# A four-layer hybrid decoder trunk on one core: recurrent mixer reordered, half of the attention's output weights left unsplit, convolution taps shared out anew

## The chip, the core and the metric

The kernel runs on one core of one Trainium2 chip. The metric is device time in microseconds (us) of one execution. The core has a matrix engine (PE, with its weight loads shown apart as PEld), a vector engine (DVE), an activation engine (ACT), a GpSimd engine (POOL) and a queue that issues transfers (SP). Each engine works through its own instructions in order; semaphores tie them together.

## What is computed

The input is x, 256 tokens by 1024 channels, batch 1. Each of four layers does

```
x = x + 0.5 * SwiGLU_1(RMSNorm(x))
x = x + Mixer(RMSNorm(x))
x = x + 0.5 * SwiGLU_2(RMSNorm(x))
```

The mixers are, in layer order, a recurrent block, forgetting attention, a causal convolution module, and a recurrent block again. SwiGLU has 2816 hidden channels. The recurrent mixer makes gate and u by one projection, runs a causal 4-tap convolution over u, computes two sigmoid gates per channel from 128x128 blocks, a decay a and a drive b, the scan h[t] = a[t] h[t-1] + b[t], and projects h * gelu(gate) out. The attention has 16 heads of 64 channels, an RMS norm on each head's q and k, and a bias from cumulated log forget gates. The convolution module gates one half of a projection by the sigmoid of the other, applies a causal depthwise convolution of 31 taps, a layer norm and a silu, and projects out.

## The kernel before, in words

**Layout.** Channels lie on the 128 partitions and tokens run along a row: x is four tiles of [128, 2, 256] (eight groups of 128 channels). Sublayer norms are folded in: products run on x times the norm's weight, and 1/rms is applied to the result.

**Weights and Feed (lines 62 to 151).** All weights come as one stream of 1 MB chunks of [128, 2048], in the order of use. A normal chunk is loaded to `wr` (3 buffers) and split in two pieces of 1024 columns: `high` (line 109, ACT) writes a rounded part `wh`, `low` (line 112, DVE) the rest `wl` (5 buffers each). Products with split operands are sums of hi*hi, hi*lo and lo*hi (lines 318, 320, 341, 373). A chunk in `whole` (lines 92 to 98) is loaded straight into a `wh` buffer and used unsplit by line 367, one matmul in place of three. `PLAIN = (0, 2)` says for which mixers (0 recurrent, 1 attention, 2 convolution) the first two of four output chunks are whole. `fill(lag)` prepares chunks until there are 5 - lag ahead of use, each piece high then low; `high(lag)` begins one chunk at most, issues both highs and returns a function that issues both lows; `steps` does one piece at a time. The load of chunk i+4 is issued after the last low of chunk i. SP carries all loads in that order.

**Start (lines 177 to 193).** x and the first chunk arrive in pieces. For each of four x tiles ACT makes the rounded x (line 233) and its square (236), DVE the rest (241) and the sum of squares (247). The sum is needed after the first 16 matmul pairs (norm_stat, line 284).

**SwiGLU (ffn, line 415)** is the bulk of the time: 22 input units and 11 output chunks, eight times.

**Recurrent mixer (rg, line 585).** Eight input units (`in_unit`, 48 matmuls each): units 0 to 3 give u, 4 to 7 the gate. Python order is the order on every engine. After unit j come `lift` (597, DVE), `first_tap` (602, ACT), `taps` (608, DVE), `gates` (615 PE, 616 and 618 ACT), `decay` (625, 626, 628, ACT), `recip` (633 to 638 DVE, 639 ACT); then two square roots (706) and the gelus (655) on ACT, `drive` (648 and the scans of 650, DVE). `finish` (731) multiplies gate and h (716, DVE), splits the last four products, and runs the output projection: units k = 0 to 3 use the whole chunks (367), 4 to 7 split ones (373), with `feed.fill(1)` after each k.

**Attention (fox, line 773).** Values first (822), then q and k pair by pair (units 0 to 5), evacuated by ACT (883 to 885). Head norms: `qk_stat` (890) multiplies the 512 squares by a selector of 32 columns, `qk_rows` (894, ACT) copies the rows out, `qk_turn` transposes them (899) and computes 1/rms on DVE. `heads` (1027) runs eight heads as a pipeline of scores, softmax (944 to 950), normalise (963), transposes (970), product with v (981, 983) and y (988 ACT, 989 DVE). The first eight heads have units 6 and 7 woven in on PE (`late_qk`), and weight pieces on ACT and DVE (`side`, one piece per step from step 3). The second eight have output units 2 to 4 woven in. A unit's result sits in one of three banks (`pr`), which the bias tiles of later heads use in turn.

**Convolution (conv, line 1079).** Eight input units. Channel tiles 4 to 7 are convolved on PE as 31 products with diagonal matrices (1127; ACT makes them, 1093), tiles 0 to 3 on DVE (1116, 1119). The loop at line 1182 issues rounds of six PE taps and five DVE taps. When tile 0 is done its mean over channels is taken (1188, PE), and from then on tiles are centred (1166), squared (1170) and summed on PE (1176). After the last sum come the variance and two table switches on ACT, then the output projection through `finish`.

Of the kernel before, what the change touches and what calls it, by code (L numbers as in the profile page):

```python
# [9 lines left out]
F32 = mybir.dt.float32  # L10
# [7 lines left out]
P = 128  # L18
# [21 lines left out]
PLAIN = (0, 2)  # L40
PE_TILES = (4, 5, 6, 7)
# [112 lines left out]
class Trunk:  # L154
# [3 lines left out]
    def build(self, pools):  # L158
# [23 lines left out]
        feed.load(RAW)  # L182
        nc.sync.dma_start(self.vec[:, KD:], self.ap["vec"][:, KD:])
# [37 lines left out]
    def prep_hi(self, b, s, js=(0, 1)):  # L221

        nc = self.nc
        if 0 in js:
            if b == 0:
# [4 lines left out]
            self.sq[b] = self.work.tile([P, 2, T], F32, tag="sq", bufs=2,  # L230
                                        name=f"sq{s}_{b}") if b else self.acc
        for j in js:
            nc.scalar.activation(self.xp[b][:, j, 0], self.x[b][:, j], AF.Copy,  # L233
                                 scale=self.v(f"norm{s}", 2 * b + j))
        j = slice(js[0], js[-1] + 1)
        nc.scalar.activation(self.sq[b][:, j], self.x[b][:, j], AF.Square)

    def prep_lo(self, b, s, js=(0, 1)):
        nc = self.nc
        for j in js:  # L240
# [3 lines left out]
                                           op0=ALU.mult, op1=ALU.subtract)  # L244
        if b:
# [339 lines left out]
    def rg(self, s, slot, last):  # L585
# [14 lines left out]
        def first_tap(j):  # L600
            for n in (2 * j, 2 * j + 1):
                nc.scalar.activation(uc[:, n], up[:, n, 0:T], AF.Identity,
                                     scale=self.v(f"rcw{slot}", n), bias=self.v(f"rcb{slot}", n))
# [26 lines left out]
        def recip(g):  # L630
# [8 lines left out]
            nc.scalar.activation(ee[:, n], ee[:, n], AF.Copy, scale=2.0, bias=-1.0)  # L639
# [27 lines left out]
        low = feed.high()  # L667
        lift(0)
        first_tap(0)
        low()  # L670
# [29 lines left out]
        evac_g(1)  # L700
        recip(2)
        decay(3)
        feed.fill(1)
# [27 lines left out]
    def finish(self, stages, s, bias=None, mid=None, whole=0):  # L731
# [29 lines left out]
        for k in range(KD - 2):  # L761
# [6 lines left out]
            self.feed.fill(1)  # L768
        c(KD - 1)
        self.feed.fill(1)  # L770
        self.out_tail([ys[KD - 2], ys[KD - 1]], s, bias)

    def fox(self, s, slot, last):
# [24 lines left out]
        hsel = carve(16, P).rearrange("p (i c) -> p i c", i=4)  # L798
        nc.gpsimd.memset(hsel, 0.0)
        for i in range(4):  # L800
            nc.gpsimd.memset(hsel[0:HD, i, 2 * i:2 * i + 1], 1.0)
            nc.gpsimd.memset(hsel[HD:P, i, 2 * i + 1:2 * i + 2], 1.0)
# [84 lines left out]
        def qk_stat(b):  # L887
            if b % 4 == 0:
                stp[b // 4] = self.st().rearrange("p (j t) -> p j t", j=2)
            nc.tensor.matmul(stp[b // 4][:FPAD], hsel[:, b % 4], sqs.pop(b),  # L890
                             start=(b % 4 == 0), stop=(b % 4 == 3))

        def qk_rows(g):
            nc.scalar.copy(rows[:FPAD], stp.pop(g)[:FPAD])

        def qk_turn(g, ps):
            ps = ps.rearrange("p j (t c) -> p (j t) c", t=TT)
            for i in range(2 * TT):
                nc.tensor.transpose(ps[:, i], rows[:, i // TT, (i % TT) * P:(i % TT + 1) * P],
                                    self.ident)  # L900
            z = self.tmp([P, 2, TT, 8], "qz")
            nc.vector.tensor_tensor(z, ps[:, :, :8].rearrange("p (j t) h -> p j t h", j=2),
                                    r2[:, None, :, None].to_broadcast([P, 2, TT, 8]), op=ALU.mult)
# [428 lines left out]
```

## Time and profile before

| | us |
|---|---|
| three runs: median (lowest to highest) | 1980.83 (1979.49 to 1981.73) |
| the profiled execution, its own time | 1979.21 |
| its span | 1977.5 |
| PE busy in the span | 1937.5 |
| DVE busy | 1440.4 |
| ACT busy | 1087.5 |

The span is what the engines' instructions cover; the profiled execution's own time is 1.7 us longer. Starts are counted from the start of the span. Matmuls are pipelined: a matmul's duration overlaps its neighbours, so the pace is read from one start to the next. An fp32 matmul that is not split shows as two instructions.

### The profile page before, as it was taken

Reading aid. Unit: us, or ns where it says so; the run is one execution under the profiler, and the core shown is the slowest. Engines: PE = TensorE matmul, PEld = TensorE weight load, DVE = VectorE, ACT = ScalarE, POOL = GpSimd, SP = SyncE. Lnnn points to the kernel's source line nnn. Section 1 sums busy time; section 2 is a strip of 40 time slices with the busy share of each in tenths; the row PEclk is TensorE's granted clock in tenths of the full one; section 3 lists DMA queues with packets and bytes.
Section 4 is the critical chain, followed back from the end, with each engine's and each line's share of the span. In section 5 each row is a group of like instructions: output and inputs, shape, how many; then the busy total and the mean of one; then the engine's idle time right before and its main releaser. Section 6 shows DMA issues by size and latency. Waiting matters only on the chain.

```text
span 1977.5 us, 28976 instructions
## 1 busy us (share of the span) xinstructions
PE 1937.5 (98%) x11450; PEld 1702.2 (86%) x11450; DVE 1440.4 (73%) x2538; ACT 1087.5 (55%) x1922; POOL 5.5 (0%) x25
## 2 busy tenths in 40 slices
PE   8999999999999998999999999989999999989999
PEld 7888988888888876888888889878888888988888
DVE  8985788767875667877587757858757876778773
ACT  6654666545654445656455546456545664566551
POOL 0000000000000000000000000000000000000000
PEclk9999999999999999999999999999999999999999
DMA  7655435545555323455555544015554554535551
GB/s 261 213 205 200 150 137 206 191 170 192 196 189 193 151 85 107 149 192 192 192 173 190 194 167 176 17 64 213 188 190 163 205 192 173 190 149 184 180 192 63
DMA packets 48665, 337.82 MB, mean 171 GB/s; under 512 B 5521, under 2 KB 6673, under 8 KB 8081
## 3 DMA queue, kind: packets, MB, share of 16 engines
q1 hardware_dynamic: 48528, 335.97, 47.2%
q8 instruction: 89, 1.46, 0.3%
q14 instruction: 48, 0.39, 0.1%
HBM read 334.90 MB, written 1.05 MB: 170 GB/s over the span
## 4 chain that ended last, share of the span: by engine, by line
PE 89%; DVE 6%; ACT 4%; issue 1%; DMA 0%; SPq 0%; ACTq 0%; DVEq 0%
PE b L318 49%; PE b L320 25%; PE b L341 4%; PE b L373 3%; PE b L1127 2%; DVE wl L112 2%; PE b L367 2%; PE b L822 1%; DVE s L1119 1%; ACT wh L109 1%; ACT s L1093 0%; ACT s L626 0%; PE b L890 0%; ACT s L625 0%; PE b L1176 0%
## 5 line engine op out<-in xcount | busy, mean ns | idle before, releaser
L318 PE MATMUL b<-xp,wh 128*128 128x512 f32 x2816 | 989.9, 396 | 7.2 <-ACT wh L109 7.2
L112 DVE TENSOR_TENSOR wl<-wr,wh 128x1024 fp32r<-128x1024 f32 (+1 forms) x622 | 743.8, 1216 | 191.6 <-ACT wh L109 191.3
L320 PE MATMUL b<-xp,wl 128*128 128x256 f32 x2816 | 790.5, 281 | 1.0 <-DVE wl L112 1.0
L109 ACT ACTIVATE wh<-wr 128x1024 fp32r<-128x1024 f32 (+1 forms) x622 | 635.7, 1047 | 165.5 <-PE b L318 83.8
L318 PEld LDWEIGHTS b<-xp,wh 128*128 128x128 f32 x2816 | 528.6, 188 | 130.5 <-ACT wh L109 7.5
L320 PEld LDWEIGHTS b<-xp,wl 128*128 128x128 f32 x2816 | 532.6, 189 | 2.6 <-DVE wl L112 2.6
L318 PE MATMUL b<-y,wh 128*128 128x512 f32 x1408 | 495.3, 395 | 0.0
L320 PE MATMUL b<-y,wl 128*128 128x256 f32 x1408 | 396.0, 281 | 0.0
L318 PEld LDWEIGHTS b<-y,wh 128*128 128x128 f32 x1408 | 264.5, 188 | 62.9
L441 ACT ACTIVATE bc<-b 128x256 f32<-128x256 f32 x352 | 117.4, 381 | 296.3 <-PE b L320 296.3
L320 PEld LDWEIGHTS b<-y,wl 128*128 128x128 f32 x1408 | 264.8, 188 | 0.0
L449 DVE TENSOR_TENSOR gu<-b,bc 128x256 f32<-128x256 f32 x352 | 132.8, 419 | 149.4 <-ACT bc L441 149.4
L341 PE MATMUL b<-xp,wh 128*128 128x256 f32 x1024 | 189.8, 287 | 5.1 <-ACT s L885 5.1
L341 PEld LDWEIGHTS b<-xp,wh 128*128 128x128 f32 x1024 | 160.1, 192 | 9.5 <-ACT s L885 6.0
L341 PE MATMUL b<-xp,wl 128*128 128x256 f32 x512 | 145.1, 283 | 0.0
L450 DVE TENSOR_TENSOR gu<-gu,ry 128x512 f32<-128x512 f32 x176 | 121.8, 692 | 6.0
L233 ACT ACTIVATE xp<-x,vec 128x256 fp32r<-128x256 f32 x96 | 46.7, 506 | 126.6 <-DVE x L494 105.3
L494 DVE SCALAR_TENSOR_TENSOR x<-b,x 128x256 f32<-128x256 f32 x128 | 53.2, 422 | 84.4 <-PE b L320 82.2
L453 ACT ACTIVATE sg<-gu 128x256 f32<-128x256 f32 x176 | 73.7, 419 | 51.2 <-DVE gu L450 41.7
L341 PEld LDWEIGHTS b<-xp,wl 128*128 128x128 f32 x512 | 98.1, 192 | 0.0
L433 DVE TENSOR_TENSOR y<-h,y 128x256 fp32r<-128x256 f32 x176 | 73.7, 419 | 3.9 <-ACT y L430 3.9
L462 DVE TENSOR_TENSOR h<-sg,gu 128x256 f32<-128x256 f32 x176 | 73.7, 418 | 1.0
(212 smaller groups left out, 1229.7 us busy)
## 6 DMA issues: line engine op xcount, KB each, us to landing
wr<-w SPq DMA_DIRECT2D x308, 1024.0 KB, 4.8
wh<-w SPq DMA_DIRECT2D x6, 1024.0 KB, 4.9
s<-wg SPq DMA_DIRECT2D x2, 1024.0 KB, 7.6
x<-xT SPq DMA_DIRECT2D x4, 256.0 KB, 5.9
wr<-w SPq DMA_DIRECT2D x4, 256.0 KB, 5.4
wr<-w SPq DMA_DIRECT2D x2, 512.0 KB, 7.5
out_dram<-x SPq DMA_DIRECT2D x8, 128.0 KB, 1.9
vec<-vec SPq DMA_DIRECT2D x1, 265.0 KB, 9.0
```

The source lines that it names most:

```text
L109: nc.scalar.activation(hi[:, c], raw[:, c], AF.Copy)
L112: nc.vector.tensor_tensor(lo[:, c], raw[:, c], hi[:, c].bitcast(F32), op=ALU.subtract)
L318: mm(bank, hi, y.rearrange("p a t -> p (a t)"), start=first, stop=False, skip_group_check=True)
L320: mm(bank[:, :T], lo, y[:, 0], start=False, stop=last, skip_group_check=True)
L341: nc.tensor.matmul(ps[:, j], w[:, k, j], m, start=(k == 0 and j == 0 and i == 0), stop=(k == KD - 1 and i == 2), skip_group_check=True)
L373: self.nc.tensor.matmul(self.o[m // 2][:, m % 2], wt[:, m * P:(m + 1) * P], mv, start=(first and m % 2 == 0 and i == 0), stop=(last and i ...
L433: nc.vector.tensor_tensor(ys[p][:, 1], hs.pop(p), ys[p][:, 0].bitcast(F32), op=ALU.subtract)
L441: nc.scalar.activation(bc[:, j], ps[j][:, T:], AF.Copy)
L449: nc.vector.tensor_tensor(gu[:, j], ps[j][:, :T], bc[:, j], op=ALU.add)
L450: nc.vector.tensor_tensor(gu, gu, self.r_b[:, None, :].to_broadcast([P, 2, T]), op=ALU.mult)
L453: nc.scalar.activation(sg, gu[:, 0], AF.Silu)
L462: nc.vector.tensor_tensor(h, sg, gu[:, 1], op=ALU.mult)
```

## The change

- `PLAIN` becomes (0, 1, 2): the first two output chunks of the attention are whole too. Its y of units 0 to 3 is one copy (ACT), without the DVE subtraction.
- Head norms: the squares become the stationary operand, 128 tokens at a time, and a selector of two columns the moving one. The sums come out token by token, DVE reads them straight from PSUM; `qk_rows` and the transposes go. `qk_turn(0)` moves from unit 5 to the end of unit 4, `qk_turn(1)` ahead of output unit 0.
- Convolution: PE takes tiles 5, 6, 7, 4 in this order, and of tile 4 the last 10 taps only; DVE takes the first 21, woven into tiles 2 and 3. DVE adds the two halves. A round has seven DVE taps, and a PE tile that ends in a round is centred a round later.
- Recurrent mixer: gates 0 and 1 follow unit 2 together, gates 2 follow unit 3, gates 3 unit 4. `first_tap` of j = 2, 3 and line 639 move from ACT to DVE. Weight chunks are begun at other points.
- `finish` prepares at most one chunk per k, both highs ahead of both lows; the attention's fills change alike.
- Start: a 1-element Copy on ACT first; squares and their sums after all four x tiles.

```diff
-PLAIN = (0, 2)
-PE_TILES = (4, 5, 6, 7)
+PLAIN = (0, 1, 2)
+PE_TILES = (5, 6, 7, 4)
+SHARED = 21
...
+        warm = self.tmp([P, 1], "warm")
+        nc.vector.memset(warm, 0.0)
+        nc.scalar.activation(warm, warm, AF.Copy)
...
         for b in range(4):
-            self.prep_hi(b, 0)
+            self.prep_hi(b, 0, squares=False)
             first[b][0]()
-            self.prep_lo(b, 0)
+            self.prep_lo(b, 0, squares=False)
             first[b][1]()
+        for b in range(4):
+            self.square(b, 0)
+            self.add_square(b)
...
+                if j < 2:
+                    nc.scalar.activation(uc[:, n], up[:, n, 0:T], AF.Identity, scale=w, bias=bias)
+                else:
+                    nc.vector.tensor_scalar(uc[:, n], up[:, n, 0:T], w, bias, op0=ALU.mult,
+                                            op1=ALU.add)
...
-            nc.scalar.activation(ee[:, n], ee[:, n], AF.Copy, scale=2.0, bias=-1.0)
+            nc.vector.tensor_scalar(ee[:, n], ee[:, n], 2.0, -1.0, op0=ALU.mult, op1=ALU.add)
...
         ps[1] = self.in_unit(wide)
-        low = feed.high()
         lift(0)
         first_tap(0)
-        low()
         lift(1)
         first_tap(1)
         taps(0)
         taps(1)
         ps[2] = self.in_unit()
-        pair_gates(0)
         low = feed.high()
         lift(2)
+        pair_gates(0)
+        pair_gates(1)
+        low()
         first_tap(2)
-        low()
         taps(2)
+        feed.high()()
         decay(0)
         ps[3] = self.in_unit()
-        pair_gates(1)
-        low = feed.high()
         lift(3)
+        pair_gates(2)
         first_tap(3)
+        taps(3)
         recip(0)
-        taps(3)
         decay(1)
         ps[4] = self.in_unit()
-        pair_gates(2)
-        low()
+        low = feed.high()
+        pair_gates(3)
         evac_g(0)
         recip(1)
+        low()
         decay(2)
-        feed.fill(1)
         ps[5] = self.in_unit()
-        pair_gates(3)
+        feed.high()
+        decay(3)
+        recip(2)
         evac_g(1)
-        recip(2)
-        decay(3)
-        feed.fill(1)
         recip(3)
...
             b(k + 2)
-            self.feed.fill(1)
+            self.feed.high()()
...
+            g, i = divmod(b, 4)
+            if i == 0:
+                stp[g] = self.st()[:, 32 * g:32 * g + 32].rearrange("p (j t h) -> p j t h", j=2,
+                                                                    t=TT)
+            sq = sqs.pop(b)
+            for j in range(2):
+                for tt in range(TT):
+                    nc.tensor.matmul(stp[g][:, j, tt, 2 * i:2 * i + 2],
+                                     sq[:, j, tt * P:(tt + 1) * P], hsel, start=True, stop=True)
...
+                if b < 4:
+                    ys[b] = self.tmp([P, T], "yp", 4)
+                    nc.scalar.activation(ys[b], ps, AF.Copy)
+                    return
...
         qk_stat(7)
-        qk_rows(1)
+        qk_turn(1)
         self.open_out()
-        first = self.out_steps(0, ys.pop(0))
-        pump(first, 4)
-        qk_turn(1, self.st().rearrange("p (j t) -> p j t", j=2))
-        pump(first, 9)
+        self.out_unit(0, ys.pop(0))
...
+        for k in range(SHARED):
+            dve_order.insert(2 * CK + 3 * k, (4, k))
...
+            if n == 4:
+                nc.vector.tensor_tensor(cv[:, n], cv[:, n], src, op=ALU.add)
+                src = cv[:, n]
...
-            new = run(ge, 6) + run(gd, 5)
+            new = run(ge, 6)
+            got = run(gd, 7)
             stats()
```

## Rows read from the trace of the kernel before

**Rows 1.** The page, part 1: busy time, share of the span, instructions, by engine.
```profile
PE 1937.5 (98%) x11450; PEld 1702.2 (86%) x11450; DVE 1440.4 (73%) x2538; ACT 1087.5 (55%) x1922; POOL 5.5 (0%) x25
```

**Rows 2.** Windows by stage: length, busy us of each engine, granted clock, DMA share, GB/s.
```profile
196.04:282.85 86.81, 81.92 (x583) 78.40 (x583) 68.01 (x118) 57.23 (x94) 0.00 (x0) 0.96 0.40 146
283.00:654.30 371.30, 371.30 (x2125) 324.56 (x2124) 273.03 (x438) 203.62 (x345) 0.00 (x0) 1.00 0.52 188
654.33:810.70 156.37, 148.42 (x960) 120.53 (x958) 104.38 (x293) 75.86 (x166) 4.13 (x15) 0.98 0.30 108
1182.34:1328.65 146.31, 136.90 (x834) 125.59 (x833) 101.59 (x224) 82.01 (x196) 0.00 (x0) 0.97 0.24 87
1700.23:1786.90 86.67, 80.94 (x583) 77.47 (x583) 68.00 (x118) 57.21 (x94) 0.00 (x0) 0.98 0.39 146
```

**Rows 3.** Timeline of PE around its waits [idle before, releaser].
```profile
254.54 17.00 PE L367 MATMUL b<-s,wh 128*128 128x256 f32 x64 [4.89 <-DVE s L716]
...
1758.74 15.77 PE L367 MATMUL b<-s,wh 128*128 128x256 f32 x64 [4.90 <-DVE s L716]
...
745.03 0.80 PE L341 MATMUL b<-xp,wh 128*128 128x256 f32 x2 [5.09 <-ACT s L885]
...
762.22 0.65 PE L981 MATMUL b<-s,s 128*64 128x256 f32 x2 [1.19 <-DVE yp L989]
...
1249.78 0.70 PE L1188 MATMUL b<-s,ones 128*128 128x256 f32 x2 [2.56 <-DVE s L1119]
1250.32 7.03 PE L1127 MATMUL b<-s,s 128*128 128x256 f32 x24
...
1294.20 0.70 PE L1176 MATMUL b<-s,ones 128*128 128x256 f32 x2 [0.58 <-DVE s L1166]
...
1301.62 15.71 PE L367 MATMUL b<-s,wh 128*128 128x256 f32 x64 [6.27 <-ACT s L1224]
```

**Rows 4.** The chain of waits: start, length, what.
```profile
271.54 11.31 PE b L373 x96
...
692.12 0.97 PE b L890 x2
...
1236.66 13.08 DVE s L1119 x33
...
1268.58 12.96 PE b L1127 x60
```

**Rows 5.** Timeline of DVE in the first recurrent mixer, 237 to 254 us.
```profile
237.75 0.69 DVE L645 TENSOR_TENSOR s<-b,ry 128x512 f32<-128x512 f32 x1 [2.15 <-PE b L615]
...
244.67 0.69 DVE L635 SCALAR_TENSOR_TENSOR s<-s,s 128x512 f32<-128x512 f32 x1 [2.87 <-ACT s L628]
...
249.88 1.22 DVE L648 TENSOR_TENSOR s<-s,s 128x1024 f32<-128x1024 f32 x1 [3.06 <-ACT s L706]
251.13 2.44 DVE L650 TENSOR_TENSOR_SCAN s<-s,s 128x256 f32<-128x256 f32 x4
```

**Rows 6.** Groups by line and shape, DVE: busy us, mean ns, idle before.
```profile
L112 DVE TENSOR_TENSOR wl<-wr,wh 128x1024 fp32r<-128x1024 f32 x618 | 741.1, 1220 | 191.0 <-ACT wh L109 190.7
...
L638 DVE TENSOR_TENSOR s<-s,s 128x512 f32<-128x512 f32 x8 | 5.5, 692 | 0.3
...
L1116 DVE TENSOR_SCALAR s<-s,vec 128x256 f32<-128x256 f32 x4 | 1.2, 351 | 0.0
```

**Rows 7.** Timeline of DVE in the attention's first eight heads.
```profile
740.68 1.23 DVE L112 TENSOR_TENSOR wl<-wr,wh 128x1024 fp32r<-128x1024 f32 x1 [0.22 <-ACT wh L109]
```

**Rows 8.** Timeline of PE around the token sums of a norm; weight loads by line.
```profile
201.64 0.50 PE L284 MATMUL b<-ones,acc 128*128 128x2 f32 x4
202.00 0.48 PE L341 MATMUL b<-xp,wh 128*128 128x256 f32 x2
...
L284 PEld LDWEIGHTS b<-ones,acc 128*128 128x128 f32 x48 | 6.5, 190 | 0.5
```

**Rows 9.** The chain of waits at the start of the span.
```profile
2.65 5.59 DMA x<-xT
```

More of the change, by code (lines that the diff above doesn't have):

```diff
@@ L219, in v, with prep_hi @@
         return self.vec[:, o + i:o + i + 1]
-    def prep_hi(self, b, s, js=(0, 1)):
+    def prep_hi(self, b, s, js=(0, 1), squares=True):
         nc = self.nc
@@ L234, in prep_hi, with square, prep_lo @@
                                  scale=self.v(f"norm{s}", 2 * b + j))
+        if squares:
+            self.square(b, s, js)
+    def square(self, b, s, js=(0, 1)):
+        if 0 in js:
+            self.sq[b] = self.work.tile([P, 2, T], F32, tag="sq", bufs=2,
+                                        name=f"sq{s}_{b}") if b else self.acc
         j = slice(js[0], js[-1] + 1)
-        nc.scalar.activation(self.sq[b][:, j], self.x[b][:, j], AF.Square)
-    def prep_lo(self, b, s, js=(0, 1)):
+        self.nc.scalar.activation(self.sq[b][:, j], self.x[b][:, j], AF.Square)
+    def prep_lo(self, b, s, js=(0, 1), squares=True):
         nc = self.nc
@@ L244, in prep_lo, with add_square @@
                                            op0=ALU.mult, op1=ALU.subtract)
+        if squares:
+            self.add_square(b, js)
+    def add_square(self, b, js=(0, 1)):
+        nc = self.nc
         if b:
@@ L767, in finish @@
             b(k + 2)
-            self.feed.fill(1)
+            self.feed.high()()
         c(KD - 1)
-        self.feed.fill(1)
+        self.feed.high()()
         self.out_tail([ys[KD - 2], ys[KD - 1]], s, bias)
@@ L797, in fox @@
                                     base=0, channel_multiplier=1)
-        hsel = carve(16, P).rearrange("p (i c) -> p i c", i=4)
+        hsel = carve(16, 2)
         nc.gpsimd.memset(hsel, 0.0)
-        for i in range(4):
-            nc.gpsimd.memset(hsel[0:HD, i, 2 * i:2 * i + 1], 1.0)
-            nc.gpsimd.memset(hsel[HD:P, i, 2 * i + 1:2 * i + 2], 1.0)
+        nc.gpsimd.memset(hsel[0:HD, 0:1], 1.0)
+        nc.gpsimd.memset(hsel[HD:P, 1:2], 1.0)
         rows = self.tmp([P, 2, T], "sq", 2)
@@ L887, in qk_stat, with qk_turn @@
         def qk_stat(b):
[L888 to L900, printed above, removed]
+            g, i = divmod(b, 4)
[7 more added lines that the diff above has]
+                                     sq[:, j, tt * P:(tt + 1) * P], hsel, start=True, stop=True)
+        def qk_turn(g):
             z = self.tmp([P, 2, TT, 8], "qz")
-            nc.vector.tensor_tensor(z, ps[:, :, :8].rearrange("p (j t) h -> p j t h", j=2),
-                                    r2[:, None, :, None].to_broadcast([P, 2, TT, 8]), op=ALU.mult)
+            nc.vector.tensor_tensor(z, stp.pop(g), r2[:, None, :, None].to_broadcast([P, 2, TT, 8]),
+                                    op=ALU.mult)
             nc.vector.tensor_scalar(z, z, 1.0 / HD, EPS, op0=ALU.mult, op1=ALU.add)
@@ L1007, in fox @@
         for b in range(6):
-            ps = self.in_unit({2: lambda: qk_turn(0, self.bank(2))} if b == 5 else None)
+            ps = self.in_unit()
             qk_evac(b, ps)
-            if b not in (4, 5):
-                feed.fill(1)
+            feed.high()()
             if b == 0:
@@ L1015, in fox @@
                 qk_stat(b - 1)
+            if b == 4:
+                qk_turn(0)
             if 1 <= b <= 4:
                 bias_pair(2 * b - 2, self.bank(b % 2))
-            if b == 4:
-                qk_rows(0)
         k_norm(0, [flat(f"o{i}", T) for i in range(4)])
@@ L1086, in conv @@
         room = [t[:, j * P:(j + 1) * P] for t in S[2:] for j in range(KD * PADC // P)]
-        pe_order = [(n, k) for n in PE_TILES for k in range(CK)]
+        pe_order = [(n, k) for n in PE_TILES for k in range(SHARED if n == 4 else 0, CK)]
         nd = [0]
@@ L1157, in conv @@
                 run(gd, 2)
-        done, pend, todo = 0, [], []
+        pend, todo = [], []
         cb = self.tmp([P, T], "cb")
@@ L1179, in stats @@
             pend.clear()
-        known = False
+        known, fresh, halves = False, [], 0
         while nst[0] < KD:
-            new = run(ge, 6) + run(gd, 5)
+            new = run(ge, 6)
+            got = run(gd, 7)
             stats()
-            todo += new
+            halves += got.count(4) + new.count(4)
+            for tiles in (got, new):
+                if 4 in tiles:
+                    tiles.remove(4)
+            if halves == 2:
+                new, halves = new + [4], 0
+            todo, fresh = todo + got + fresh, new
             if not known and 0 in todo:
```

16 lines of the change are left out of this document (7 added, 9 removed).

## The prediction, made before the changed kernel was run

> **What bounds the kernel now.** I read the page's busy shares first: PE is busy 1937.5 of 1977.5 us [rows 1], so only two things can shorten the run much, its 40 idle us and work that it needn't do or does slowly. The windows by stage come next. From one mixer to the next PE is busy 371.30 of 371.30 us at full clock [rows 2]: the SwiGLU stages are PE's own work, and the change leaves them alone. The four mixers hold 86.81, 156.37, 146.31 and 86.67 us, with granted clocks of 0.96 to 0.98 [rows 2]. The timeline of PE then shows where: 4.89 and 4.90 us ahead of the first output product of either recurrent mixer, 5.09 and 1.19 in the attention, 2.56 and 6.27 in the convolution [rows 3]. After a long wait the matmuls that follow run slowly. 64 instructions of line 367 took 17.00 us in the first recurrent mixer [rows 3]; the same kind of instruction (unsplit, 256 columns) in mid-convolution took 12.96 for 60, 0.216 each [rows 4], which makes 13.8 for 64. So the wait of 4.89 cost 3.2 us more at the lower of the clock's two levels (1.2 and 2.4 GHz), and in the second such mixer 15.77 - 13.8 = 1.9 more.
>
> **Recurrent mixers.** PE's work before the output projection ends at 254.54 - 4.89 = 249.65 us. The first product of line 716 is late because DVE had to wait 2.15, 2.87 and 3.06 us for gates, decay and square root [rows 5], 8.1 in sum: gates came late on PE, and ACT stood at line 639, waiting for DVE, before it could go on to the next decay. The new order issues all gates by the end of unit 4, and line 639 moves to DVE, so ACT never waits for DVE in mid-recip; I take these 8.1 us as gone. In exchange DVE gets four first taps at 0.35 (line 1116, same operation and size) and four scalings of 512 columns, which the trace doesn't show on DVE: between 0.35 (half the columns) and 0.69 (line 638, the same columns, two operands) [rows 6]. I take 0.5, nearer to the same operation; that is 1.4 + 2.0 = 3.4 us, bounds 2.8 to 4.2. DVE's end goes from 254.54 to about 249.9, PE waits some 0.3 us, and no slow stretch follows. Two pieces of a chunk (2 x 1.22 [rows 6]) also move from before unit 2 to after it; I take them as lying where DVE had waited for that unit, bounds 0 to 2.4. In the output projection the old order split three chunks after k = 0 in one go; now there is one per k, 2.4 us of DVE against 3.5 us of PE for an unsplit k (16 x 0.216) and 2.8 for a split one (11.31 / 4 [rows 4]), so the later products have their operands. On SP the two whole chunks go out one and two steps later, behind the load of the first split output chunk; their buffers were free after units 3 and 4, 10 us and more ahead of use. Work of PE in the mixer: 81.92 - 3.2 = 78.7; with the 0.3, 79.0. That saves 86.81 - 79.0 = **7.8** and 86.67 - 79.0 = **7.7** us. Bounds per mixer: 8.1 (no wait), or 2 (a wait of 3 us with its slow stretch).
>
> **Attention.** Unsplit weights cost PE time: 32 products at 2 x 0.216 = 0.43 in place of three at 11.31 / 96 = 0.118, 0.35 [rows 4]. That is +0.08 each, +2.6 in all, and on the path, since PE is full around them. What they spare is two chunks of splitting and four subtractions on ACT and DVE. The 5.09 us wait doesn't go with that: the woven steps still split a chunk at steps 3 and 4, now the next one, and there DVE itself waited for ACT's high (0.22 [rows 7]) before the scores behind which unit 6's evacuation stands. From step 7 on no pieces are left and y is one copy, so the 1.19 us, a wait for the subtraction [rows 3], goes: 1.2 (bounds 0 to 1.2). The head sums: one product took 0.97 us per pair [rows 4]; the nearest row to the new ones is line 284, the same operands, four instructions in 202.00 - 201.64 = 0.36 us [rows 8]. Eight of these are 0.72 per pair, -0.25 for seven pairs (the eighth falls into the wait): -1.75. Two times four transposes (line 899) go, taken at the same 0.09 each: -0.7. Sum: 2.6 - 1.2 - 1.75 - 0.7 = **-1.1**, bounds +0.2 to -8 (the 5.09 goes after all, with a slow stretch priced below at 1.85). The moved `qk_turn(0)` puts its small DVE steps ahead of one bias pair; PE's in-unit 5 covers them. The whole chunks leave ACT and DVE without work in units 4 and 5, and SP only waits there for buffers that units 3 and 4 free.
>
> For those sums a rule stands against the edit. The Trainium skill, "TensorE: Matmul & The Clock Gate", section "Step-by-step: what each phase is for", says that a weight load's time scales with the number of stationary columns, and these go from 32 to 128. The trace shows 190 ns for such a load [rows 8]; eight of them unhidden would be 1.5 us per pair, +4.4 in place of -1.75. Four such loads and their products fitted into 0.36 us, so they overlap, and the sum goes by that.
>
> **Convolution.** PE drops 21 of 124 taps, 21 x 0.43 = 9.1 us, but not all of it is on the path. Tile 0 is DVE's and is done at 1249.78 [rows 3] whatever PE does, as the taps ahead of it are the same. With five taps a round PE had issued 42 of its taps by then; with seven a round it has issued 30, and waits 12 x 0.43 = 5.2 us longer, 7.8. After that 73 taps are left in place of 82: 9 x 0.43 = 3.9 less. The old end also held a wait of 0.58 for the last tile's centring [rows 3]; now three other tiles' sums stand behind the last tap and hide the addition of tile 4's halves, its centring and its square: 4.5 less. DVE has then 83 taps at 13.08 / 33 = 0.40 [rows 4], eight centrings and the addition at no more than 0.5, 37 us. PE has 73 taps and eight times two sums of the same form, 89 x 0.43 = 38 us, and the slow stretch of 1.85 (24 instructions in 7.03 us, 5.18 at 0.216 each [rows 3, 4]), 40 us: DVE hides, by 3 us. The longer wait may lengthen that stretch by 0 to 1.3 (the one behind 4.89 us cost 3.2): I take 0.4. **-4.1**, bounds -4.5 to 0 (if DVE is the bound). The 6.27 us for variance and table loads stay.
>
> **Start.** Squares leave ACT's way and a table load comes earlier, but the second x tile lands only at 2.65 + 5.59 = 8.24 us [rows 9], and the first unit can't close before the same squares are summed, now behind everything else: 0, bounds -1 to +0.5.
>
> **Sum.** 7.8 + 7.7 + 1.1 + 4.1 = 20.7 us. The profiled execution took 1979.21, so it would take 1958.5; the median of the runs shown is 1.6 higher, which makes **1960**.
>
> **The rivals.** A is the forecast: 1956 to 1964, chance 0.60.
> B: the recurrent mixers' wait shrinks but stays. If the moved pieces count in full, DVE is 2.4 later and PE waits about 2.7 us. A wait of 2.56 was followed by a slow stretch [rows 3], so the clock's loss would stay: 2 x 2.2 in place of 15.5, about 1971. The DVE count is within 1 us of PE's end, which speaks for it; that nothing else is moved onto DVE speaks against. 0.16.
> C: the 5.09 us wait in the attention closes as well, 5.09 and 1.85 more: 1953. For it: DVE loses four subtractions, one of them right there; against: ACT's high ends no earlier. 0.08.
> D: the weight loads of the head sums (190 ns each) aren't hidden: 4.4 + 1.75 = 6.2 us above A, 1966. This trace's overlap speaks against it; 0.04. The same page's rule, taken alone, would have it so.
> E, on the other side: DVE becomes the bound. Its waits in the recurrent mixers stay 8.1 us because the order among them is set by ACT's decays and not by line 639; the added work of up to 4.2 us comes on top, and in the convolution DVE's 83 taps set the end. Then each recurrent mixer is 4.2 longer, the convolution gains nothing and the attention costs 0.2: 1980.8 + 8.6 = 1989.4. It decides if DVE's end falls after 254.5 us. For it: DVE is busy 68 of 86.8 us there [rows 2], no little; against: ACT is the one that was waited for. 0.06.
> F: the edits do as they say but the time only moves, the first mixers' waits turning up in the output projection (late chunks on the one-per-k plan) and in the attention: within 4 us of now. 0.06.
>
> **How the numbers follow.** About 0.2%, 4 us, is what a measurement of this kernel can tell from no change. Faster by more: A, B, C and D, 0.88; within: F, 0.06; slower: E, 0.06. The likeliest case gives 1960. The range takes in A, C, D and B: 1952 to 1972; E, F and the outer bounds are left out.
>
> **What would show it.** Right: no PE wait over 1 us ahead of line 367 in either recurrent mixer and 13.8 us for its 64 instructions; windows of about 79, 155, 142 and 79 us for the mixers; a PE wait near 7.8 us ahead of the convolution's mean; the 5 us wait in the attention still there. Wrong: line 716 (DVE) still releasing the first output product after 2 us or more; PE waiting for DVE at the end of the convolution's taps; eight head-sum instructions taking 1 us or more per pair.

## The result, and the profile after

The changed kernel takes 1946.49 us (median of 4 runs, 1945.12 to 1948.06), the kernel before in the same comparison 1981.18 us: a ratio of 0.9827, 95% interval 0.981 to 0.9844. That is 34.7 us faster. The forecast was 1960, with a range from 1952 to 1972: the sign is right, the size is 13.5 us short, and the range missed it by 5.5.

Page of the changed kernel, part 1, to be held against [rows 1]:

```profile
PE 1911.9 (98%) x11416; PEld 1698.4 (87%) x11416; DVE 1448.4 (75%) x2569; ACT 1069.4 (55%) x1880; POOL 3.8 (0%) x19
```

PE has 34 instructions less, yet it is 25.6 us less busy. The whole span, of one profiled execution each, lost 33.7 us (1977.5 to 1943.8), so only some 8 us came from idle time of PE. The windows by stage of the changed kernel show where (length, busy us of PE, PEld, DVE, ACT, POOL, granted clock, DMA share, GB/s); they answer to [rows 2]:

```profile
196.52:274.32 77.80, 77.80 (x583) 75.32 (x583) 70.65 (x127) 53.86 (x86) 0.00 (x0) 1.00 0.44 163
274.32:643.38 369.06, 369.06 (x2125) 325.64 (x2125) 273.16 (x439) 203.54 (x345) 0.00 (x0) 1.00 0.53 189
643.38:797.44 154.06, 148.06 (x968) 125.57 (x967) 98.68 (x286) 71.57 (x160) 2.44 (x9) 0.98 0.30 110
1166.48:1308.65 142.17, 128.11 (x791) 117.94 (x791) 110.05 (x246) 75.78 (x175) 0.00 (x0) 0.94 0.24 89
1677.72:1755.52 77.80, 77.80 (x584) 75.32 (x583) 70.61 (x127) 53.86 (x86) 0.00 (x0) 1.00 0.44 163
```

The mixers do about what was forecast: 77.80, 154.06, 142.17 and 77.80 us against "about 79, 155, 142 and 79". The second row is the surprise. The stage of two SwiGLU blocks between the first two mixers took 371.48 us before (282.85 to 654.33 in [rows 2]) and takes 369.06 now, with PE busy for all of it at full clock both times and not one instruction of it changed. Each of the three such stretches is 2.4 us shorter, and the last SwiGLU block, behind the last mixer, 2.3 (190.6 to 188.3): 9.6 us, most of the gap.

The timeline of PE in the changed kernel has these waits of a microsecond and more in the mixers [idle before, releaser], and the chain of waits (start, length, what) these stretches; they answer to [rows 3] and [rows 4]:

```profile
731.73 0.79 PE L358 MATMUL b<-xp,wh 128*128 128x256 f32 x2 [5.10 <-ACT s L903]
...
1233.70 1.22 PE L1217 MATMUL b<-s,ones 128*128 128x256 f32 x2 [8.74 <-DVE s L1137]
1280.32 16.82 PE L384 MATMUL b<-s,wh 128*128 128x256 f32 x64 [5.32 <-ACT s L1253]
```

```profile
248.99 13.81 PE b L384 x64
...
681.24 0.79 PE b L913 x8
...
752.13 7.01 PE b L384 x32
```

Line 384 is the old line 367. Ahead of it there is no wait left in either recurrent mixer and its 64 products take 13.81 us, as said. The wait of the attention stands (5.10, was 5.09); that of the convolution is 8.74 where 7.8 was forecast.

What the SwiGLU stages lost is pace. Groups by line of PE, first of the kernel before, then of the changed one (busy us, mean ns of one | idle before):

```profile
L318 PE MATMUL b<-xp,wh 128*128 128x512 f32 x2816 | 989.9, 396 | 7.2 <-ACT wh L109 7.2
...
L318 PE MATMUL b<-y,wh 128*128 128x512 f32 x1408 | 495.3, 395 | 0.0
```

```profile
L335 PE MATMUL b<-xp,wh 128*128 128x512 f32 x2816 | 981.3, 391 | 7.0 <-ACT wh L110 7.0
...
L335 PE MATMUL b<-y,wh 128*128 128x512 f32 x1408 | 494.7, 395 | 0.0
```

One such product is recorded until after the next pair has begun, so its busy time has no holes, and divided by the count it is the time of a pair (512 columns with the high weights, 256 with the low): 989.9 / 2816 = 351.5 ns before, 981.3 / 2816 = 348.5 now. Pairs that move y, in the same loop with the same weights, stay at 351.8 and 351.3. And the kernel before was not uniform. In the stretches 330 to 390 us (behind a mixer) and 500 to 560 us (ahead of one) its groups read

```profile
L318 PE MATMUL b<-xp,wh 128*128 128x512 f32 x171 | 60.5, 399 | 0.0
```

```profile
L318 PE MATMUL b<-xp,wh 128*128 128x512 f32 x174 | 60.4, 391 | 0.0
```

353.8 and 347.1 ns a pair: all SwiGLU blocks behind a mixer were slow, all ahead of one fast. In the changed kernel both stretches are at 347 ns:

```profile
L335 PE MATMUL b<-xp,wh 128*128 128x512 f32 x175 | 60.7, 390 | 0.0
```

```profile
L335 PE MATMUL b<-xp,wh 128*128 128x512 f32 x174 | 60.4, 390 | 0.0
```

DVE, ACT and the DMAs do the same in these stages in both kernels.

### The profile page after: what moved, and what is told of

Its sections match the earlier page's. It is cut to its first block, busy times and chain, and to the rows that moved or that the text cites. A ratio compares the mean times of both kernels' runs of the same rounds, so it can differ in the third digit from the quotient of the medians.

```text
span 1943.8 us, 28888 instructions
## 1 busy us (share of the span) xinstructions
PE 1911.9 (98%) x11416; PEld 1698.4 (87%) x11416; DVE 1448.4 (75%) x2569; ACT 1069.4 (55%) x1880; POOL 3.8 (0%) x19
## 3 DMA queue, kind: packets, MB, share of 16 engines
HBM read 334.90 MB, written 1.05 MB: 173 GB/s over the span
## 4 chain that ended last, share of the span: by engine, by line
PE 94%; DVE 3%; ACT 2%; DMA 0%; issue 0%; SPq 0%; DVEq 0%; ACTq 0%
PE b L335 49%; PE b L337 26%; PE b L358 7%; PE b L384 3%; PE b L390 2%; PE b L1146 2%; PE b L840 1%; DVE s L1137 1%; DVE wl L113 1%; PE b L636 1%; ACT wh L110 1%; ACT s L1109 0%; PE b L1198 0%; PE b L997 0%; DMA x<-xT 0%; PE b L321 0%
## 5 line engine op out<-in xcount | busy, mean ns | idle before, releaser
L335 PE MATMUL b<-xp,wh 128*128 128x512 f32 x2816 | 981.3, 391 | 7.0 <-ACT wh L110 7.0
L358 PE MATMUL b<-xp,wh 128*128 128x256 f32 x1024 | 184.7, 283 | 5.1 <-ACT s L903 5.1
```

The source lines that it names most:

```text
L335: mm(bank, hi, y.rearrange("p a t -> p (a t)"), start=first, stop=False, skip_group_check=True)
L358: nc.tensor.matmul(ps[:, j], w[:, k, j], m, start=(k == 0 and j == 0 and i == 0), stop=(k == KD - 1 and i == 2), skip_group_check=True)
```

## Experiments: is it where xp lies?

The change reserves its [128, 1] tile `warm` ahead of acc and xp. Tiles are laid out in steps of 32 bytes, so in every partition xp0 moves from byte 122432 to 122464; the weights (wh from 38464) and the six slabs with y (y0 at 170368) stay. Theory P: this place sets the pace. Rival Q: the instructions do, or what runs beside them.

```diff
 (kernel before)
         feed.load(RAW)
+        self.tmp([P, 1], "warm")
```

> The kernel before with one edit: a tile of [128, 1] under the name `warm` is reserved as the first tile of the work pool, with no instruction on it; it moves acc, sq and xp by 32 bytes in each partition (xp0 from 122432, a multiple of 64, to 122464). Theory P (place): products that move xp run faster in the changed kernel because its `warm` tile shifts xp by 32 bytes. Then line 318 and 320 on xp go from 351.6 ns a pair to about 348.5 (2816 pairs, -8.7 us), line 341 loses about 5.5 us over its 1536 instructions, and the time is about 1967 (1965 to 1969), with every wait of before still there. Rival Q (work): the pace comes from what the other engines do or from the order of the instructions; then nothing changes, 1981 (1979 to 1983) and 351.6 ns a pair.

The padded kernel before (e1): 1972.29 us, ratio 0.995 (0.9936 to 0.9965). Two windows of it, the first recurrent mixer and the stage behind:

```profile
195.76:282.24 86.48, 80.79 (x584) 77.14 (x583) 68.04 (x118) 57.30 (x94) 0.00 (x0) 0.96 0.39 147
282.24:651.28 369.04, 369.04 (x2126) 325.81 (x2125) 273.09 (x438) 203.49 (x345) 0.00 (x0) 1.00 0.53 189
```

No instruction was added, and the SwiGLU stages are those of the changed kernel. P holds for them, Q falls. But 9.0 us came, not 14: the recurrent mixer lost 0.3 us only. Its products on xp are faster too, but there DVE's late line was still waited for (5.62 us ahead of the output products, 4.89 before), and the gain turned into waiting. The attention and the convolution got no shorter either: 158.78 and 147.80 us in this execution, 156.53 and 146.31 before, with granted clocks of 0.97 and 0.95 against 0.98 and 0.97.

```diff
 (changed kernel)
-        warm = self.tmp([P, 1], "warm")
+        warm = self.slab.tile([P, KD * PADC], F32, tag="s0", bufs=1, name="warm0")[:, :1]
```

> The changed kernel with its early `warm` column taken from the slab of y0 in place of a tile of its own, so that acc, xp0 and xp1 lie where the kernel before has them (xp0 at 122432) and xp2, xp3 4096 bytes, a whole tile, below; every instruction of the change stays. Theory P (place): the SwiGLU stages behind a mixer go back to 353 ns a pair on xp (371.5 us from mixer to mixer in place of 369.05), line 358 to 120.0 ns each in place of 116.8, all of it on the path now that PE no longer waits in the recurrent mixers: rg stages 79.0, and the time is 1960 (1957 to 1962), which is what the forecast gave from the change's own steps. Rival Q (work): the change's instructions, not the place, make the pace; then 1946.5 (1945 to 1948). Rival R: the FFN's 9.7 us go back, the in-units' don't: 1956.

The changed kernel with xp0 and xp1 in their old place (e5; xp2 and xp3 lie a tile lower, at the same distance modulo 128): 1960.70 us (1958.00 to 1962.05), ratio 0.9896 (0.988 to 0.9912): P, and near the forecast's own number. All instructions of the change are in it. Windows of the first recurrent mixer, the stage behind it, the attention and the convolution:

```profile
198.91:277.65 78.74, 78.74 (x584) 76.25 (x583) 70.54 (x126) 53.76 (x86) 0.00 (x0) 1.00 0.44 161
277.65:649.13 371.48, 371.48 (x2126) 324.69 (x2125) 273.19 (x438) 203.77 (x346) 0.00 (x0) 1.00 0.52 188
649.13:805.63 156.50, 150.52 (x968) 128.10 (x967) 98.65 (x285) 71.51 (x160) 2.45 (x9) 0.96 0.29 108
...
1177.11:1319.30 142.19, 129.13 (x792) 118.96 (x791) 110.03 (x245) 75.71 (x175) 0.00 (x0) 0.95 0.24 89
```

So the place made 9.0 us of difference to the kernel before and 14.2 to the changed one. Not all of the 14.2 is the pace. Of the 16.5 us between the two profiled executions 9.6 lie in the SwiGLU blocks behind mixers, 1.9 in the recurrent mixers and some 2.5 ahead of the first mixer, where e5's first block ran slow though that of the kernel before ran fast. The last 2.4 lie in the attention, at a granted clock of 0.96 where the changed kernel had 0.98; that isn't the place, as a slow place (e2 below) has 153.76 us there. Next, which place, and against what? A control moves everything behind xp and sq by the same 32 bytes, xp not:

```diff
 (kernel before, behind the loop that makes the first xp)
             first[b][1]()
+        self.tmp([P, 1], "warm")
```

> The kernel before with the [128, 1] tile reserved behind xp and sq: nz, bc, gu, sg, h and the mixers' y pairs move by 32 bytes, acc, sq, xp, the weights and the slabs don't. P, it is xp's place against the weights that counts: 1981 (1979 to 1983), SwiGLU stages 371.5 from mixer to mixer. Rival S, it is the place of what ACT and DVE read and write beside PE: as with the pad ahead of xp, 1972.

The control (e7): 1980.07 us, ratio 0.9994 (0.9985 to 1.0004): no difference. What ACT and DVE work on in the SwiGLU stages is not it.

In the changed kernel a second tile ahead of `warm` moves xp by another 32 bytes and the slabs with it; one in the constants' pool moves the weights too:

```diff
 (changed kernel, first run)
+        self.tmp([P, 1], "pad")
         warm = self.tmp([P, 1], "warm")
 (changed kernel, second run)
+        c.tile([P, 1], F32, name="pad")
         warm = self.tmp([P, 1], "warm")
```

> The changed kernel with a second [128, 1] tile reserved ahead of `warm`: xp moves by another 32 bytes, back onto a multiple of 64 (122496), and the slabs behind the work pool (the SwiGLU's y pairs) move by 32 too, off a multiple of 64 (170400). P: products on xp go back to 351.6 ns a pair, +14 us; if the place counts for y as it does for xp, the 1408 pairs that move y gain 3.1 ns each, -4.4: 1956 (1954 to 1958), or 1960 if y is indifferent. Q: 1946.5 (1945 to 1948).

> The changed kernel with a [128, 1] tile reserved in the constants' pool, ahead of everything but x and vec: identity, weights, xp and slabs all move by 32 bytes, so that xp lies on a multiple of 64 again (122496), weights and y off it. P1, a product's pace is set by the place of the moved operand alone: pairs on xp 351.6, pairs on y 348: +14 - 4.4, 1956 (1954 to 1958). P2, it is set by the distance between weights and moved operand: all distances are as in the changed kernel, 1946.5 (1945 to 1948), pairs on xp 348.5. Q: 1946.5 as well, so P2 and Q are told apart by the other three runs.

The first (e2) took 1962.82 us (ratio 0.9902, 0.9887 to 0.9917), the second (e4) 1946.39 us (0.9819, 0.9802 to 0.9835). In both xp and y lie on the same bytes; only the weights differ. Groups by line of e2, then of e4:

```profile
L336 PE MATMUL b<-xp,wh 128*128 128x512 f32 x2816 | 1000.5, 397 | 6.5 <-ACT wh L110 6.5
...
L336 PE MATMUL b<-y,wh 128*128 128x512 f32 x1408 | 491.9, 393 | 0.0
```

```profile
L336 PE MATMUL b<-xp,wh 128*128 128x512 f32 x2816 | 981.8, 391 | 7.1 <-ACT wh L110 7.1
...
L336 PE MATMUL b<-y,wh 128*128 128x512 f32 x1408 | 494.7, 395 | 0.0
```

355.3 and 348.7 ns on xp, 349.4 and 351.3 on y. It is the distance between weights and moved operand (P2), not the operand's own place (P1): e4 moves both and has the changed kernel's paces again. My number for the first run, 1956, was too low, since I had taken a shift of 64 bytes for none.

How the distance counts was tried with more shifts: of xp and the slabs on the kernel before, of the slabs alone on the changed one.

```diff
 (kernel before; 64, 96 and 160 bytes ahead of xp)
+        self.tmp([P, 1], "pad"); self.tmp([P, 1], "warm")
+        self.tmp([P, 1], "pad"); self.tmp([P, 1], "pad2"); self.tmp([P, 1], "warm")
+        self.tmp([P, 25], "pad"); self.tmp([P, 1], "warm")
 (changed kernel; slabs by 32 and by 64 bytes)
+        self.slab.tile([P, 1], F32, tag="pad", bufs=1, name="pad")
+        self.slab.tile([P, 16], F32, tag="pad", bufs=1, name="pad")
```

> The kernel before with two [128, 1] tiles reserved at the head of the work pool, no instruction on them: xp0 at 122496, a multiple of 64 as in the kernel before (122432) and as in the run with the second pad; the slabs move by 32 bytes, as there. If being a multiple of 64 decides, xp pairs are slow again: 1981 less 4 for y, 1977 (1975 to 1982), SwiGLU stages at 353 ns a pair either behind each mixer only (as in the kernel before) or everywhere (as in the run with the second pad, then 1984). Rival: any shift breaks up what the kernel before happens to have; then as with one pad, 1972 less up to 3, 1969 to 1973.

> The kernel before with three [128, 1] tiles reserved at the head of the work pool, no instruction on them: xp0 at 122528, off a multiple of 64 as with one pad (122464), the slabs moved by 64 (170432). If half a line of 64 bytes between weights and moved operand is all that counts, xp is fast and y slow as with one pad: 1972 (1970 to 1974), 347 ns a pair in every SwiGLU stage, 369.05 us from mixer to mixer. Rival: finer or coarser places count; then another pace than 347, 353 or the mixture of the kernel before.

> The kernel before with 160 bytes reserved at the head of the work pool and no instruction on them: xp0 at 122592, which lies to 128 bytes as 122464 does (one pad, 347 ns a pair everywhere); the slabs move by 128. If places count modulo 128, this is the run with one pad again: 369.05 us from mixer to mixer, 347 ns a pair on xp, 351.1 on y, 1972 (1970 to 1974). Rival, a longer period: another pace, as with three pads, and a time of 1976 to 1986.

> The changed kernel with a [128, 1] tile reserved as the first of the slab pool: only the slabs move, by 32 bytes (y pairs from 170368, a multiple of 64, to 170400); xp and the weights stay where the changed kernel has them. P: pairs on xp keep 348.5 ns, pairs on y go from 351 to about 348, -4.4 us, and other products that move slabs gain a little: 1941.5 (1940 to 1943). Q: 1946.5 (1945 to 1948).

> The changed kernel with the slabs moved by 64 bytes in place of 32 (y pairs from 170432, a multiple of 64 as in the changed kernel), xp and weights unmoved. If the place modulo 64 is what counts for y, pairs on y take 351.1 ns again as in the changed kernel, and the time is 1946.5 (1945 to 1948). Rival, any move of the slabs helps: 349.3 ns and 1943.5.

The times, in us, and ratios: 64 bytes (e6) 1985.59, 1.0022 (1.0012 to 1.0032); 96 bytes (e10) 1981.35, 1.0003 (0.9993 to 1.0012); 160 bytes (e14) 1970.76, 0.9945 (0.9928 to 0.9961); slabs by 32 (e3) 1943.51, 0.9809 (0.9794 to 0.9823); slabs by 64 (e12) 1946.47, 0.9825 (0.981 to 0.984). The runs sort by the distance from weights to operand modulo 128 bytes (the weight tiles lie alike in this count; pace of a pair as busy / count over the whole run; for y the distance is that of the first slab, y0; "before" and "after" are the kernels before and after the change):

```
distance   pairs on xp, ns                                  pairs on y, ns, by the place of y0
  0        351.5 (before), 351.7 (e7), 352.5 (e5)           351.5 (e10), 351.5 (e12)
 32        348.5 (e1, after, e12), 348.2 (e14),             none
           348.7 (e4), 348.8 (e3)
 64        354.6 (e6), 355.3 (e2)                           351.3 (e1, after, e4), 351.6 (e14)
                                                            351.8 (before, e5, e7)
 96        352.1 (e10)                                      349.5 (e3), 349.4 (e2, e6)
```

The y column mixes two distances. A slab takes 8 x 286 x 4 = 9152 bytes (line 419 of the kernel before), which is 64 more than a multiple of 128, so y1, y3 and y5 lie 64 bytes off from y0, y2 and y4 in this count. Taken apart, by the mean time from the start of one pair on y to the next (without the last 16 pairs of a block, which are taken in another order), the slabs read

```
run (place of y0, of y1)      y0, y2, y4, ns            y1, y3, y5, ns
after (64, 0)                 352.4, 352.5, 348.8       349.9, 351.1, 352.5
e12   (0, 64)                 350.8, 353.1, 350.9       351.0, 352.2, 348.7
e3    (96, 32)                352.2, 352.7, 350.3       346.5, 346.8, 346.4
before (64, 0)                353.1, 352.4, 348.8       351.5, 351.1, 352.5
e14   (64, 0)                 352.9, 348.9, 351.9       351.1, 353.1, 350.5
```

At 32 y is fast, as xp is (347.6 in the same measure); the slabs' shift by 32 gained it on three slabs of six, so the run fell short of the 348 ns and the 1941.5 us that were expected. A shift by 64 only exchanges the two groups' distances, so e12 couldn't tell 64 from 0. e4 has the changed kernel's paces slab by slab, within 0.1 ns. Elsewhere the distance modulo 128 doesn't settle the pace: e14 has every slab 128 bytes further than the kernel before, and y2 went from 352.4 to 348.9.

My "modulo 64" is refuted by xp at 32 and 96 (the run with 96 bytes was to be at 1972); with 64 bytes every SwiGLU block was slow, and the time 1.6 us above the 1984 that I had for this case. And the 160 bytes, predicted from the period of 128 before they ran, came out like 32 for xp: the window of that run between the first two mixers reads

```profile
282.95:652.11 369.16, 369.16 (x2126) 324.19 (x2125) 273.17 (x438) 203.76 (x346) 0.00 (x0) 1.00 0.53 189
```

Distance 0 alone has two paces, 347 and 353, by the stage (the two rows of the kernel before, 330 to 390 and 500 to 560 us); in e5, at the same distance, the first block was slow too. What puts a stage into one or the other was not tried, nor why a distance matters at all. The best layout found moves the slabs by 32 bytes: the stages between mixers are at 368.4 us and the time at 1943.51. Its interval overlaps that of the changed kernel, so the 3 us in the total are not shown; the pace of y is. Slabs of a size that is a multiple of 128, all at 32, would be worth some 4 us by an estimate from e3's row (12 of 22 y, 768 pairs, 5.1 ns each); that was not run.

## Experiments: the change's own parts

**Scaling back on ACT.** One edit of the recurrent mixer undone:

```diff
 (changed kernel, recip)
-            nc.vector.tensor_scalar(ee[:, n], ee[:, n], 2.0, -1.0, op0=ALU.mult, op1=ALU.add)
+            nc.scalar.activation(ee[:, n], ee[:, n], AF.Copy, scale=2.0, bias=-1.0)
```

> The changed kernel with one of the recurrent mixer's edits undone: the scaling by 2 and -1 at the end of each recip goes back from DVE to ACT. If that move is what lets ACT run ahead (my step: ACT stood there, waiting for DVE, before it could go on to the next decay), part of DVE's 8.1 us of waiting comes back: PE waits 2 us or more ahead of line 384, its 64 instructions take 15 us or more, the recurrent stages take 81 to 87 us in place of 77.8 and the time is 1953 to 1965. Rival: the order of gates and decays did it alone; PE is the bound, the stages stay at 77.8 and the time at 1946.5 (1945 to 1948).

1959.38 us, ratio 0.9893 (0.9878 to 0.9909), 12.9 above the changed kernel. Timelines of PE and of DVE in the first recurrent mixer:

```profile
252.74 16.83 PE L384 MATMUL b<-s,wh 128*128 128x256 f32 x64 [3.90 <-DVE s L735]
```

```profile
232.98 0.69 DVE L656 SCALAR_TENSOR_TENSOR s<-s,s 128x512 f32<-128x512 f32 x1 [1.33 <-ACT s L649]
...
239.61 0.69 DVE L656 SCALAR_TENSOR_TENSOR s<-s,s 128x512 f32<-128x512 f32 x1 [1.61 <-ACT s L649]
...
248.07 1.23 DVE L669 TENSOR_TENSOR s<-s,s 128x1024 f32<-128x1024 f32 x1 [3.06 <-ACT s L725]
```

And ACT, at the scalings of the first and the last group:

```profile
229.54 0.63 ACT L660 ACTIVATE s<-s 128x512 f32<-128x512 f32 x1 [3.76 <-DVE s L659]
...
245.04 0.63 ACT L660 ACTIVATE s<-s 128x512 f32<-128x512 f32 x1 [2.17 <-DVE s L659]
```

ACT stands behind DVE, DVE waits for ACT's decays and roots again ([rows 5] had 2.87 and 3.06 there), PE waits 3.90, the products behind take 3.0 us more than 13.81, and the stage takes 84.71 us. In the changed kernel none of these waits is there. So the new order of the gates needs this edit: without it the change is worth some 2 us a mixer (86.81 to 84.71, the place included), not 9. Whether the scaling's move would do without the new order was not run.

**The attention's unsplit weights**, taken out of the change, and put alone into the kernel before:

```diff
 (changed kernel: out; kernel before: the reverse)
-PLAIN = (0, 1, 2)
+PLAIN = (0, 2)
...
-                if b < 4:
-                    ys[b] = self.tmp([P, T], "yp", 4)
-                    nc.scalar.activation(ys[b], ps, AF.Copy)
-                    return
```

> The changed kernel with one of the attention's edits undone: the two chunks of its out projection are split again, and the first four y are pairs (three products of 0.118 us in place of two of 0.216). My terms for this edit: +2.6 for the slower form, -1.2 for a wait that went; undone, the attention goes from 154.05 to 152.7 us and the time to 1945.1 (1943.5 to 1946.5). Rival: the splitting that it spares ACT and DVE is worth more than the product time, and waits come back: the attention takes 156 us or more, the time is 1948 to 1952.

> The kernel before with one of the attention's edits alone: weights of the first half of its out projection unsplit and the first four y copied whole, everything else (the planned loads and splits, the head sums, the rest of the change) as before. My term: +2.6 for 32 products in the slower form, -1.2 for a wait that goes, so the attention from 156.5 to 157.9 us and the time from 1981 to 1982.4 (1981 to 1984). Rival, from the run with the split put back (which cost 7.6 us): the spared splitting is worth more than the products cost in any order of the work, and the attention falls to 150 to 154 us, the time to 1974 to 1979. Third: it is worth that only under the changed kernel's plan of whole chunks; then my term holds here and the two edits belong together.

Out: 1954.90 us, ratio 0.9865 (0.9849 to 0.9882), slower by 8.4 where 1.4 faster was expected, and 2.9 above the range of the rival that had it slower. Alone in the kernel before: 1981.70 us, ratio 1.0002 (0.9993 to 1.0011), no difference. Window of the attention, a wait of PE and what DVE did ahead of it, in the run with the split put back:

```profile
645.30:806.98 161.68, 150.73 (x1000) 129.23 (x999) 104.93 (x293) 75.43 (x164) 2.45 (x9) 0.95 0.30 105
```

```profile
715.87 1.97 PE L937 MATMUL b<-ident,s 128*128 128x128 f32 x8 [4.24 <-DVE s L931]
```

```profile
706.37 2.36 DVE L113 TENSOR_TENSOR wl<-wr,wh 128x1024 fp32r<-128x1024 f32 x2 [3.21 <-ACT wh L110]
708.65 0.18 DVE L918 TENSOR_TENSOR qz<-b,r 128x32 f32<-128x32 f32 x1
...
713.25 2.36 DVE L113 TENSOR_TENSOR wl<-wr,wh 128x1024 fp32r<-128x1024 f32 x2 [0.42 <-ACT wh L110]
715.53 0.89 DVE L931 COPY s<-rqk 128x256 f32<-128x256 f32 x4
```

The third theory of that pair fits: the change plans one whole chunk per unit, and without unsplit chunks those of units 4 and 5 put 2.36 us of splitting each on DVE, one ahead of the head norms' first step (line 918), one right ahead of the norm's scales (line 931) that the first heads wait for; in the changed kernel DVE splits nothing there. PE is idle 10.95 us in this attention, 6.00 in that of the changed kernel; the rest of the 7.6 us is slower products, at a granted clock of 0.95. The unsplit weights don't pay by themselves; the plan needs them. That the two splits make all of the loss is argued from this trace, not tried.

**More taps on DVE**, on top of the slabs' better place:

```diff
 (changed kernel with the slabs moved by 32 bytes)
-SHARED = 21
+SHARED = 25
```

> A candidate: the changed kernel with the slabs moved by 32 bytes (as in the run with the slab pad, 1943.5) and four more taps of tile 4 on DVE (SHARED 25 in place of 21). DVE waits 2.3 us for PE's last tap in the changed kernel; four taps are 1.7 us of PE and 1.6 of DVE, so the two end about together. Theory (PE's end sets the convolution's, as my forecast had it): the convolution's stage goes from 142.2 to 140.5 or 141.2 us, the time to 1942 (1940.5 to 1944). Rival (DVE is the bound from here): the stage takes 142.2 to 144, the time is 1943.5 to 1946.

1944.34 us, ratio 0.9812 (0.9797 to 0.9827). The convolution's window:

```profile
1168.04:1309.47 141.43, 126.81 (x784) 116.28 (x783) 111.60 (x249) 74.35 (x171) 0.00 (x0) 0.94 0.25 90
```

That is 1.05 us less than the same layout with 21 (142.48), as the theory wanted, but with 21 the stage took anything from 141.07 (e12) to 142.48 by layout. Inconclusive, and no better in total.

## Why the forecast fell short

**The step that failed** is in the first paragraph of the prediction: "the SwiGLU stages are PE's own work, and the change leaves them alone". The instructions were left alone; their operands were not. I priced the early `warm` by its table load and not by the 32 bytes that its tile takes, and no rival had it that untouched work runs at another pace. The term that I put at nothing measured 9.6 us in the SwiGLU blocks behind mixers and 1.9 in the recurrent mixers; with the 1.4 by which the attention's term was too small this is 12.9 of the missing 13.5. With xp put back the change takes 1960.70 us, 0.7 from the forecast. That nearness is in part luck: in e5's execution the first block lost 3.0 us against the kernel before and the attention, at the lower granted clock, gained nothing. A pace of 353.8 and one of 347.1 ns for the same products stood in the trace of before; a reading by halves of a stage would have asked what sets them.

**Recurrent mixers**, -7.8 and -7.7: right, and for the reason given. At the old place the stages took 78.74 and 78.75 (79.0 forecast, of them 0.3 of a wait that didn't come); the new place takes 0.94 more off each. That the scaling's move is needed for it is shown by the run without it. Rival B (a wait that stays) didn't come.

**Attention**, -1.1: the stage went from 156.53 us ([rows 2] stops 0.16 before its end) to 154.06 at a granted clock of 0.98 both times, -2.5. The place has no visible part in that: at this clock the changed kernel's code takes 153.76 to 154.06 us with xp at 32 (e3, e8) and at 64 (e2), that of the kernel before 156.45 at 64 (e6) and 157.03 at 0 (e7). At granted clocks of 0.96 and 0.97 both take some 2.3 us longer (e4 156.25, e5 156.50; e1 158.78). So the term was too small, though within its bounds: PE's idle time in the stage fell from 7.95 us to 6.00, its busy time from 148.6 to 148.06. Of the single terms, a pair's head sums take 0.79 us (0.72 forecast, 0.97 before), so rival D's exposed loads are excluded (its 4.4 us counts eight pairs where the sum counts seven; with seven it is 3.9). The wait of 1.19 is gone, and of two small ones beside it, 0.42 and 0.56, 0.43 and 0.36 are left; the 5.10 stayed, so rival C is out. The term of +1.4 for unsplit weights and their wait is within what the run of the edit alone allows (-1.4 to +2.2), but the sum treated it as separable. Taking it out of the change costs 8.4 us.

**Convolution**, -4.1: 146.31 to 142.17, and 142.19 at the old place. The wait before the mean was forecast at 7.8 and is 7.74 there. At the new place it is 8.74: the products on xp ahead of it end sooner, DVE's first tile doesn't (the mean comes 67.4 us into the stage, 67.6 in e5), so the place gained nothing here. Two terms behind it were wrong and cancel: the wait of 6.27 was to stay and is 5.32, and the 64 products behind it, which the sum left alone, take 16.82 us for 15.71. That the sum is right to 0.1 us is luck to that extent.

**Start**, 0: not resolved. The first recurrent mixer's first product begins at 196.35 us in the changed kernel, at 195.88 in the kernel before, and 2.6 to 3.0 us later in e5 (198.91), where the first block ran at the slow pace. But over the other variants of the changed kernel it goes from 195.77 (e4) to 199.01 (e2), and e9, with a fast first block, has 198.44.

**Rival E** (DVE as the bound) asked for DVE's waits to stay. They stay only without the scaling's move. In the convolution DVE waits 2.32 us for PE's last tap of tile 4 in the changed kernel, so PE was the bound there.

## What to carry to other kernels

Where PE is busy all the time, read the pace of its products stage by stage, as busy time over count, before calling a stage untouched: two paces for one form are a reserve, and a change that allocates anything ahead of an operand can turn it on or off. Compare two versions only after their operands have been given the same place against the weights, or try a pad of 32 bytes by itself first. Check each tile's place, not the first one's alone: a tile size that is no multiple of 128 bytes gives neighbours different distances. And an edit that frees an engine is worth what the plan around it does with the freed time, so price it together with that plan: alone it was worth nothing here, taken out it cost 8 us.

## What the runs showed of the hardware that was not expected

Products of one form and size, at full granted clock and without waits, ran at 348.2 to 355.3 ns a pair over a run, 2%, depending on the distance in bytes between weights and moved operand within a partition. At 32 (modulo 128; xp also at 160) all were fast: 347.6 ns from start to start on xp, 346.4 to 346.8 on the slabs of y. At 0, 64 and 96 the paces were 347.9 to 354.1 and went by more than the distance modulo 128: at 0 a whole SwiGLU block on xp stays at one of two, 348 or 354, and a slab of y that moved by 128 bytes went from 352.4 to 348.9. The recurrent mixer, whose products move 256 columns each, doesn't show it between 32 and 64: with the slabs moved by 32 it took 78.02 us with xp at 32 (e3) and 78.01 at 64 (e2). The Trainium skill, "SBUF — State Buffer", section "A bandwidth-pool intuition that's wrong (but worth ruling out)", lists a read port for weight loads beside the one for the moved operand and calls it independent; by that alone their distance would not matter. The runs differ, and decide. Two single tiles of four bytes a partition, with no instruction on them, made the kernel before 0.2% slower; one made it 0.5% faster.
